# Weight parts in four homes, raw loads seven units ahead, and other distances for x's chunks in a two-layer decoder trunk

## The chip, the cores and the metric

One core of a Trainium2 chip. The metric is the time of one execution in device microseconds (us), the median of the runs shown.

## What is computed

A trunk of two layers on 256 tokens with 2048 features, all in float32. Each layer normalises its input, multiplies it with one wide matrix `w_in`, runs three token mixers on the columns of the product, projects the result of each by its own matrix, weighs the three by sigmoid gates, and adds the product with `w_out` to its input. A last normalisation closes the trunk. Cut to what the change touches:

```python
def hybrid_layer(x, norm_w, w_in, ..., w_a_out, w_b_out, w_c_out, w_out, cos, sin, top_k):
    h = rms_norm(x, norm_w)
    proj = h @ w_in
    ...
    y_b = (conformer_conv(ub, conv_w, conv_b, cln_w, cln_b) * jax.nn.silu(zb)) @ w_b_out
    ...
    g = jax.nn.sigmoid(gates).reshape(b, s, N_BRANCH, D_MODEL)
    merged = g[:, :, 0] * y_a + g[:, :, 1] * y_b + g[:, :, 2] * y_c
    return x + merged @ w_out

def reference(x, ...):
    for i in range(DEPTH):
        x = hybrid_layer(x, norm_w[i], w_in[i], ...)
    return rms_norm(x, final_norm_w)
```

## The kernel before

**Weights.** A float32 product is made of three products of reduced parts: high times high, low times high, high times low. A unit of weights is 256 rows by 512 columns. `load_unit` (L235) has SP load it raw, 512 KB, into one of four raw buffers. ACT casts it into the high part `wh` (`high`, L246), DVE subtracts that from the raw unit and has the low part `wl` (`low`, L250), and PE multiplies: twelve matmuls of 128x512 for a plain unit (L260). `wh` and `wl` have three buffers each, here called homes. A cast into a home waits until PE has used what was there.

**The two pipelines.** Twice in a layer the units are run by `run` (L480 to 510): once for the gates of the second branch with its projection `w_b_out`, and once for `w_out`. Its inner `ahead(n)` gives out the load of unit n + 4 and casts and subtracts unit n + 2, and then unit n is multiplied. Fourteen units of each pipeline come from `seven` (L418 to 476): these are half units (six matmuls) of a product of two by two blocks with seven instead of eight block products. The weights of some are sums of blocks: `fetch` (L439) has SP load the first block into a slot in two halves, and `more` (L454) has POOL add the second by an accumulating transfer. Outside of these pipelines, `unit` loads, casts and subtracts at once, with three homes.

**x's chunks at a layer's end.** The product with `w_out` is made in four quarters of 512 columns. For each quarter `ask` (L1414) has SP load the layer's input chunk, `arrive` (L1447, L1449) has DVE add the product and what `seven` kept aside, and `leave` has ACT square the chunk for the next normalisation (L612). In layer 0 `turned` then takes the chunk to the features' layout: DVE transposes blocks (L289), POOL stores them in four transfers `z` (L292), POOL loads them back as `zy` (L298, one buffer), DVE multiplies with the norm's weight (L617), ACT casts (L624), and DVE subtracts the low part (L173). How many units later the load and the multiplication come is `LATER - 2 - (q == 3)`, with LATER 10, and `least` 3. The scheduler orders the instructions of each engine by such distances and by priorities.

**Layer 1's start.** Layer 1 multiplies raw features first: its norm's factor, one number per token, is made from the squares by L630 and L519 to L524 (ACT's square root is L519), set on diagonals by L537 and L538, and spread over the partitions by two matmuls of PE (L678) in the middle of the sixth unit. The norm's square root needs another function table of ACT than the gates' sigmoids (L1366); `warm_sqrt` (L529) loads it ahead of time.

**The tail.** In layer 1 the quarters' squares give the last norm's factor. The rows of t = 0 are finished first: square root L1534, factor L1535 to L1538, rescale L1544 on DVE and L1542 on ACT, output L1545. Those of t = 1 follow with the merges L1515 and L1525.

Of the kernel before, what the change touches and what calls it, by code (L numbers as in the profile page):

```python
# [8 lines left out]
F32 = mybir.dt.float32  # L9
# [39 lines left out]
def trunk(ctx: ExitStack, tc: tile.TileContext, x, w_in, xt, w_a, w_b, w_c, w_out,  # L49
# [14 lines left out]
    def queued():  # L64
        return tc.issue_after(first[0].ins) if first[0] is not None else nullcontext()

    x0n = cp.tile([P, C_ID + S], F32, name="x0n")
    idle = tp.tile([P, P], F32, tag="dg", bufs=1, name="idle")
    nc.vector.memset(idle, 0.0)
    eps = cp.tile([P, 1], F32, name="eps")  # L70
    nc.vector.memset(eps, EPS)
# [146 lines left out]

    def load_unit(w, k0, kn, segs, dst=None):
        n = sum(c for _, c in segs)  # L220
        raw = wp.tile([P, kn, n], F32, tag="raw", bufs=4, name=nm("raw"))
        if dst is None:
            dst = (wp.tile([P, kn, n], F32R, tag=t, bufs=3, name=nm(t)) for t in ("wh", "wl"))
        count[0] += 1
        with tc.high_priority():
            o = 0
            for c0, c in segs:
                src = w[k0 * P:(k0 + kn) * P, c0:c0 + c].rearrange("(k p) c -> p k c", p=P)
                if count[0] == 1:

                    for k in range(kn):
                        nc.scalar.dma_start(raw[:, k, o:o + c], src[:, k, :])
                else:
                    with queued():
                        dma = nc.sync.dma_start(raw[:, :, o:o + c], src)  # L235
                    if count[0] <= 8:
                        first[0] = dma
                o += c
            if count[0] == 8:
                with queued():  # L240
                    first[0] = nc.sync.dma_start(cst, consts)
        return (raw, *dst)
# [137 lines left out]
    def chunk_N(w, segs, act, nk, ku=2, accs=None, ks=None, banks=False):  # L380
# [4 lines left out]
            background(token_products(accs, n, unit(w, k0, ku, segs), act, k0, ku, nk, range(NT), banks))  # L385
        return accs

    class Unit:

        size, before, now, after = 1, (), (), ()  # L390
# [4 lines left out]
    def plain(w, c0, act, k0, accs, nk, banks=False, ts=range(NT)):  # L395
# [1 line left out]
            return token_products(accs(), 512, u[1:], act, k0, 2, nk, ts, banks)  # L397

        def load():
            u = load_unit(w, k0, 2, [(c0, 512)])  # L400
            count[0] -= 1
            return u

# [17 lines left out]
    def seven(w, c0, act, sums, banks, keep):  # L421
# [19 lines left out]
        def sub(h, g, add, a, k0, t, bank):  # L441
            ts, hs = slice(t * P, (t + 1) * P), slice(h * 2, h * 2 + 2)

            def load():
                if g not in grow:
                    u = load_unit(w, 4 + h * 2, 2, [(c0, 512)])
                    count[0] -= 1
                    return u
                return (grow[g][:, hs, :],
                        *(wp.tile([P, 2, 512], F32R, tag=v, bufs=3, name=nm(v)) for v in ("wh", "wl")))  # L450

            def more():
                with tc.high_priority():
# [23 lines left out]
    def run(units, tasks):  # L477
# [3 lines left out]
        got = {}  # L481

        def ahead(n):
            if n + 4 < len(units):
                for f in units[n + 4].before:
                    f()
                got[n + 4] = units[n + 4].load()
            if 0 <= n + 2 < len(units):
                high(got[n + 2])
                low(got[n + 2])  # L490
                if units[n + 2].more:
                    units[n + 2].more()

        for n in range(-4, 0):
            ahead(n)
        for n, u in enumerate(units):
            ahead(n)
# [149 lines left out]
    for layer in range(DEPTH):  # L647
# [282 lines left out]
        hq = slot(F32R).rearrange("p a (b t) -> p (a b) t", t=P)  # L930
        for v in range(KD // 4):
            nc.scalar.copy(hq[:, v * 4:v * 4 + 4, :].rearrange("p k (w t) -> p k w t", w=2), hx[v][:, :, :, TOPK:P])
        kiT = sp.tile([P, 1, S], F32, tag="kiT", bufs=1, name=nm("kiT"))
        va = [sp.tile([P, NT, 2 * P], F32R, tag=v, bufs=1, name=nm(v)) for v in ("vah", "val")]
        wi = small(NIH, 2)
        wi2 = tp.tile([P, NIH // 2], F32, tag="wi2", bufs=1, name=nm("wi2"))
# [514 lines left out]
        def leave(q):  # L1451
            xc, c0 = xcs[q], q * 512
            x_squares([xc[:, t, :] for t in range(NT)], ssq, q, range(NT))
            if last:
                for t in range(NT):
                    nc.vector.tensor_mul(xfr[t][:, c0:c0 + 512], xc[:, t, :], fwr[:, c0:c0 + 512])
            else:
                turned([xc[:, t, :] for t in range(NT)], partial(x_parts_F, xn, c0 // P, nwn), LATER - 2 - (q == 3),
                       t4() if q == 1 else None, least=3)
                nc.scalar.dma_start(x1[:, :, c0:c0 + 512].rearrange("t p d -> p t d"), xc)  # L1460

        sums = parts(KC)
# [134 lines left out]
```

## Time and profile before

| what | value |
|---|---|
| time, median of 3 runs | 2012.91 us (2012.84 to 2014.74) |
| the profiled execution's own time | 2013.33 us |
| its span in the profile | 2011.6 us |
| PE busy | 2001.1 us, 99% of the span, 9338 matmuls |
| DVE busy | 1595.5 us, 79% |
| ACT busy | 1093.6 us, 54% |
| POOL busy | 210.1 us, 10% |
| share of PE in the chain that ended last | 97% |
| granted TensorE clock | 0.999 of full speed |
| moved by DMA | 463.80 MB, 231 GB/s in the mean |

The span runs from the first to the last record of the profile; the time has some 1.7 us around it. PE, DVE, ACT and POOL are the engines for matmuls, for vector work, for activations and copies, and for transfers with accumulation or a new layout; SP issues most loads. An answer of the timeline has, in each row, the start, the duration, the engine, the line, the operation and its tiles, how many instructions were drawn together, and in brackets how long the engine was idle before and what ended the wait.

### The profile page before, as it was taken

Reading aid. Unit: us, or ns where it says so; the run is one execution under the profiler, and the core shown is the slowest. Engines: PE = TensorE matmul, PEld = TensorE weight load, DVE = VectorE, ACT = ScalarE, POOL = GpSimd, SP = SyncE. Lnnn points to the kernel's source line nnn. Section 1 sums busy time; section 2 is a strip of 40 time slices with the busy share of each in tenths; the row PEclk is TensorE's granted clock in tenths of the full one; section 3 lists DMA queues with packets and bytes.
Section 4 is the critical chain, followed back from the end, with each engine's and each line's share of the span. In section 5 each row is a group of like instructions: output and inputs, shape, how many; then the busy total and the mean of one; then the engine's idle time right before and its main releaser. Section 6 shows DMA issues by size and latency. Waiting matters only on the chain.

```text
span 2011.6 us, 25827 instructions
## 1 busy us (share of the span) xinstructions
PE 2001.1 (99%) x9338; PEld 1677.8 (83%) x9338; DVE 1595.5 (79%) x2124; ACT 1093.6 (54%) x1261; POOL 210.1 (10%) x316
## 2 busy tenths in 40 slices
PE   9999999999999999999999999999999999999998
PEld 8889888888888888888888988888888888888876
DVE  8667899878878876677785779988889788756777
ACT  7556555565644555455564555555656445544564
POOL 0111112100010001212210111111000100012120
PEclk9999999999999999999999999999999999999999
DMA  7788678866676678979987886788666766789795
GB/s 267 230 286 263 189 226 287 246 178 179 180 223 193 182 226 236 279 225 298 290 246 233 278 249 188 234 279 249 178 177 177 221 198 190 226 247 267 235 299 169
DMA packets 235585, 463.80 MB, mean 231 GB/s; under 512 B 17280, under 2 KB 30080, under 8 KB 235328
## 3 DMA queue, kind: packets, MB, share of 16 engines
q1 hardware_dynamic: 206592, 385.06, 62.1%
q0 software_dynamic: 27200, 73.94, 13.9%
q10 hardware_dynamic: 1664, 3.15, 0.4%
q8 instruction: 73, 1.20, 0.3%
q14 instruction: 56, 0.46, 0.1%
HBM read 429.31 MB, written 32.77 MB: 230 GB/s over the span
## 4 chain that ended last, share of the span: by engine, by line
PE 97%; DMA 2%; DVE 0%; ACT 0%; issue 0%; POOL 0%; DVEq 0%; ACTq 0%; POOLq 0%
PE acc L260 84%; PE mm L260 10%; DMA raw<-in_w_out_dram 1%; PE mm L1036 1%; DMA z<-zt 1%; PE mm L1126 0%; DMA zy<-z 0%; PE mm L1094 0%; PE mm L1231 0%; PE mm L1177 0%; ACT wh L246 0%; PE mm L795 0%; PE mm L1207 0%; PE mm L1097 0%; PE mm L1006 0%; PE mm L1236 0%
## 5 line engine op out<-in xcount | busy, mean ns | idle before, releaser
L260 PE MATMUL acc<-wh,s 128*128 128x512 f32 (+1 forms) x5088 | 1259.7, 389 | 1.4 <-ACT wh L246 1.0
L246 ACT CAST wh<-raw 128x1024 fp32r<-128x1024 f32 (+1 forms) x698 | 730.8, 1048 | 767.3 <-PE acc L260 510.8
L260 PEld LDWEIGHTS acc<-wh,s 128*128 128x128 f32 x5088 | 946.9, 188 | 190.9 <-ACT wh L246 2.4
L250 DVE TENSOR_TENSOR wl<-raw,wh 128x1024 fp32r<-128x1024 f32 (+1 forms) x699 | 846.4, 1214 | 319.6 <-ACT wh L246 317.1
L260 PE MATMUL acc<-wl,s 128*128 128x512 f32 (+1 forms) x2352 | 626.2, 388 | 0.0
L260 PEld LDWEIGHTS acc<-wl,s 128*128 128x128 f32 x2352 | 440.8, 188 | 90.2 <-DVE wl L250 1.0
L292 POOL DMA_DIRECT2D z<-zt x196 | 117.6, 616 | 1250.2 <-DVE zt L289 907.6
L605 DVE SCALAR_TENSOR_TENSOR s<-yT,cst,s 128x256 f32<-128x256 f32 x480 | 212.2, 478 | 0.0
L260 PE MATMUL mm<-wh,s 128*128 128x512 f32 x480 | 123.6, 389 | 0.1
L260 PEld LDWEIGHTS mm<-wh,s 128*128 128x128 f32 x480 | 90.0, 188 | 19.2 <-ACT wh L246 0.5
L250 DVE TENSOR_TENSOR wl<-s,wh 128x1024 fp32r<-128x1024 f32 x48 | 58.5, 1219 | 18.4 <-ACT wh L246 18.1
L246 ACT CAST wh<-s 128x1024 fp32r<-128x1024 f32 x48 | 50.5, 1053 | 40.8 <-PE acc L260 22.9
L260 PEld LDWEIGHTS mm<-s,wl 128*128 128x128 f32 x512 | 66.9, 191 | 5.0
L260 PE MATMUL mm<-wl,s 128*128 128x512 f32 x240 | 68.8, 390 | 0.0
L260 PE MATMUL mm<-s,wl 128*128 128x192 f32 x512 | 66.0, 271 | 0.0
L298 POOL DMA_DIRECT2D zy<-z x50 | 36.0, 720 | 268.7 <-DMA z<-zt 140.8
L260 PEld LDWEIGHTS mm<-wl,s 128*128 128x128 f32 x240 | 45.0, 188 | 9.7 <-DVE wl L250 0.4
L289 DVE STREAM_TRANSPOSE zt<-acc 128x512 f32<-128x512 f32 (+1 forms) x68 | 45.4, 681 | 8.2 <-PE acc L260 8.2
L454 POOL DMA_DIRECT2D s<-in_w_in_dram x16 | 19.2, 1203 | 115.7 <-DVE wl L250 100.8
L543 DVE TENSOR_TENSOR s<-zy,s 128x1024 fp32r<-128x1024 f32 x20 | 24.3, 1215 | 5.1 <-ACT s L542 5.1
L542 ACT CAST s<-zy 128x1024 fp32r<-128x1024 f32 x20 | 21.0, 1048 | 11.8 <-DVE zy L593 7.0
L1313 DVE TENSOR_TENSOR ev<-acc,ev 128x512 f32<-128x512 f32 x24 | 16.5, 688 | 11.9 <-PE acc L260 11.9
(280 smaller groups left out, 1093.4 us busy)
## 6 DMA issues: line engine op xcount, KB each, us to landing
raw<-in_w_in_dram SPq DMA_DIRECT2D x539, 512.0 KB, 4.5
raw<-in_w_out_dram SPq DMA_DIRECT2D x52, 512.0 KB, 7.2
zy<-z POOLq DMA_DIRECT2D x48, 512.0 KB, 5.2
z<-zt POOLq DMA_DIRECT2D x188, 128.0 KB, 4.6
raw<-in_w_a_dram SPq DMA_DIRECT2D x32, 512.0 KB, 3.9
raw<-in_w_c_dram SPq DMA_DIRECT2D x32, 512.0 KB, 4.4
raw<-in_w_b_dram SPq DMA_DIRECT2D x32, 512.0 KB, 5.0
s<-in_w_in_dram POOLq DMA_DIRECT2D x16, 512.0 KB, 8.3
```

What stands on the lines that cost most here:

```text
L246: newest_parts[0] = nc.scalar.copy(u[1], u[0])
L250: newest_parts[1] = sub = nc.vector.tensor_sub(u[2], u[0], u[1].bitcast(F32))
L260: newest[0] = nc.tensor.matmul(o, lhsT, rhs, start=start, stop=stop, skip_group_check=True)
L289: nc.vector.transpose(tmp[:, t].rearrange("p b k i -> p k b i"), src.rearrange("p k (b c) -> p k b c", b=4, c=32))
L292: nc.gpsimd.dma_start(z[:, :, :, a, :].rearrange("t b c e -> c (t b) e"), tmp[a * 32:(a + 1) * 32].rearrange("c t b k i -> c (t b) (k i)"))
L298: nc.gpsimd.dma_start(y.rearrange("p (t a) k i -> p t (a k i)", a=4), z.rearrange("t b c a e -> (b c) t (a e)"))
L454: nc.gpsimd.dma_start(grow[g][:, hs, :], block(add, h), accum_op=ALU.add)
L542: nc.scalar.copy(h, src)
L543: nc.vector.tensor_sub(l, src, h.bitcast(F32))
L605: nc.vector.scalar_tensor_tensor(o, yT[:, c, q:q + S], wq, o, op0=ALU.mult, op1=ALU.add)
L1036: nc.tensor.matmul(ps[:, q * S:(q + 1) * S], qi[i][:, hd, :], ki[j][:, 0, :], start=n == 0, stop=n == 2)
L1313: nc.vector.tensor_mul(sg[t], y[t], sg[t])
```

## The change

Raw units have five buffers instead of four. A new helper `weight_parts` gives the two pipelines their homes: every fourth is a pair of tiles `ph`, `pl`, which other code uses in other stages, so there are four instead of three. `ahead` loads seven units ahead instead of four and converts three ahead instead of two. To make room in the on-chip memory, `x0n`, `idle` and `kiT` move into buffers whose tags other tiles have. For x's chunks the distance `LATER - 2 - (q == 3)`, which is 8, 8, 8, 7, becomes `LATER - (5, 4, 2, 3)[q]`, which is 5, 6, 8, 7, and `least` becomes 4 for the third chunk.

```diff
--- before.py
+++ after.py
@@ -64,8 +64,8 @@
     def queued():
         return tc.issue_after(first[0].ins) if first[0] is not None else nullcontext()
 
-    x0n = cp.tile([P, C_ID + S], F32, name="x0n")
-    idle = tp.tile([P, P], F32, tag="dg", bufs=1, name="idle")
+    x0n = sp.tile([P, C_ID + S], F32, tag="yT", bufs=1, name="x0n")
+    idle = tp.tile([P, P], F32, tag="sc", bufs=2, name="idle")
     nc.vector.memset(idle, 0.0)
     eps = cp.tile([P, 1], F32, name="eps")
     nc.vector.memset(eps, EPS)
@@ -218,7 +218,7 @@
 
     def load_unit(w, k0, kn, segs, dst=None):
         n = sum(c for _, c in segs)
-        raw = wp.tile([P, kn, n], F32, tag="raw", bufs=4, name=nm("raw"))
+        raw = wp.tile([P, kn, n], F32, tag="raw", bufs=5, name=nm("raw"))
         if dst is None:
             dst = (wp.tile([P, kn, n], F32R, tag=t, bufs=3, name=nm(t)) for t in ("wh", "wl"))
         count[0] += 1
@@ -385,6 +385,15 @@
             background(token_products(accs, n, unit(w, k0, ku, segs), act, k0, ku, nk, range(NT), banks))
         return accs
 
+    homes = [0]
+
+    def weight_parts():
+
+        homes[0] += 1
+        if homes[0] % 4 == 0:
+            return [v.rearrange("p (k c) -> p k c", k=2) for v in pair(1024)]
+        return [wp.tile([P, 2, 512], F32R, tag=t, bufs=3, name=nm(t)) for t in ("wh", "wl")]
+
     class Unit:
 
         size, before, now, after = 1, (), (), ()
@@ -397,7 +406,7 @@
             return token_products(accs(), 512, u[1:], act, k0, 2, nk, ts, banks)
 
         def load():
-            u = load_unit(w, k0, 2, [(c0, 512)])
+            u = load_unit(w, k0, 2, [(c0, 512)], weight_parts())
             count[0] -= 1
             return u
 
@@ -443,11 +452,10 @@
 
             def load():
                 if g not in grow:
-                    u = load_unit(w, 4 + h * 2, 2, [(c0, 512)])
+                    u = load_unit(w, 4 + h * 2, 2, [(c0, 512)], weight_parts())
                     count[0] -= 1
                     return u
-                return (grow[g][:, hs, :],
-                        *(wp.tile([P, 2, 512], F32R, tag=v, bufs=3, name=nm(v)) for v in ("wh", "wl")))
+                return (grow[g][:, hs, :], *weight_parts())
 
             def more():
                 with tc.high_priority():
@@ -481,17 +489,17 @@
         got = {}
 
         def ahead(n):
-            if n + 4 < len(units):
-                for f in units[n + 4].before:
+            if n + 7 < len(units):
+                for f in units[n + 7].before:
                     f()
-                got[n + 4] = units[n + 4].load()
-            if 0 <= n + 2 < len(units):
-                high(got[n + 2])
-                low(got[n + 2])
-                if units[n + 2].more:
-                    units[n + 2].more()
-
-        for n in range(-4, 0):
+                got[n + 7] = units[n + 7].load()
+            if 0 <= n + 3 < len(units):
+                high(got[n + 3])
+                low(got[n + 3])
+                if units[n + 3].more:
+                    units[n + 3].more()
+
+        for n in range(-7, 0):
             ahead(n)
         for n, u in enumerate(units):
             ahead(n)
@@ -930,7 +938,7 @@
         hq = slot(F32R).rearrange("p a (b t) -> p (a b) t", t=P)
         for v in range(KD // 4):
             nc.scalar.copy(hq[:, v * 4:v * 4 + 4, :].rearrange("p k (w t) -> p k w t", w=2), hx[v][:, :, :, TOPK:P])
-        kiT = sp.tile([P, 1, S], F32, tag="kiT", bufs=1, name=nm("kiT"))
+        kiT = tp.tile([P, S], F32, tag="rb", bufs=1, name=nm("kiT")).unsqueeze(1)
         va = [sp.tile([P, NT, 2 * P], F32R, tag=v, bufs=1, name=nm(v)) for v in ("vah", "val")]
         wi = small(NIH, 2)
         wi2 = tp.tile([P, NIH // 2], F32, tag="wi2", bufs=1, name=nm("wi2"))
@@ -1455,8 +1463,8 @@
                 for t in range(NT):
                     nc.vector.tensor_mul(xfr[t][:, c0:c0 + 512], xc[:, t, :], fwr[:, c0:c0 + 512])
             else:
-                turned([xc[:, t, :] for t in range(NT)], partial(x_parts_F, xn, c0 // P, nwn), LATER - 2 - (q == 3),
-                       t4() if q == 1 else None, least=3)
+                turned([xc[:, t, :] for t in range(NT)], partial(x_parts_F, xn, c0 // P, nwn), LATER - (5, 4, 2, 3)[q],
+                       t4() if q == 1 else None, least=3 + (q == 2))
                 nc.scalar.dma_start(x1[:, :, c0:c0 + 512].rearrange("t p d -> p t d"), xc)
 
         sums = parts(KC)
```

The lines of the changed kernel are eight or nine higher: L617 is L625, L439 is L448, L1414 is L1422, L1447 is L1455.

How the order moves, at three places. First SP's queue in layer 0's second pipeline: raw weight loads (L235), the two halves of a fetch (L439, L448) and the request for x's last chunk (L1414, L1422). Before:

```order
L235 DMA raw_1364_7792<-in_w_out_dram 128x2x512
L235 DMA raw_1367_7812<-in_w_out_dram 128x2x512
L1414 DMA t4_1445_8225<-in_x_dram 128x2x512
L235 DMA raw_1372_7830<-in_w_out_dram 128x2x512
L439 DMA s8_1371_7827<-in_w_out_dram 128x2x512
L235 DMA raw_1377_7860<-in_w_out_dram 128x2x512
L235 DMA raw_1382_7889<-in_w_out_dram 128x2x512
```

and now:

```order
L235 DMA raw_1362_7743<-in_w_out_dram 128x2x512
L235 DMA raw_1366_7764<-in_w_out_dram 128x2x512
L235 DMA raw_1373_7799<-in_w_out_dram 128x2x512
L448 DMA s8_1370_7794<-in_w_out_dram 128x2x512 x2
L1422 DMA t4_1442_8177<-in_x_dram 128x2x512
L235 DMA raw_1378_7829<-in_w_out_dram 128x2x512
L235 DMA raw_1384_7862<-in_w_out_dram 128x2x512
```

The ninth unit's load, raw_1372 before and raw_1373 now, stood behind the request for x's chunk; it now stands ahead of it, and both halves of the fetch stand together.

Second, DVE at the end of layer 0, from the merge of x's third chunk (t4_1429) on: weights' low parts (L250), transposes (L289), the first chunk's multiplication (L617, now L625) and low part (L173). Before:

```order
L1449 TENSOR_TENSOR t4_1429_8149<-t4_1429_8149,s8_1339_7704 128x512
L250 TENSOR_TENSOR wl_1458_8280<-raw_1456_8277,wh_1457_8279 128x1024
L289 STREAM_TRANSPOSE zt_1463_8333<-t4_1429_8149 128x4x4x32 x2
L250 TENSOR_TENSOR wl_1461_8298<-raw_1459_8295,wh_1460_8297 128x1024
L617 TENSOR_TENSOR s8_1465_8368<-zy_1452_8257,cst_75 128x1024
L250 TENSOR_TENSOR wl_1480_8416<-raw_1478_8413,wh_1479_8415 128x1024
L173 TENSOR_TENSOR s8_1466_8370<-s8_1465_8368,s8_1466_8370 128x4x256
L250 TENSOR_TENSOR wl_1483_8420<-raw_1481_8417,wh_1482_8419 128x1024
```

and now:

```order
L1457 TENSOR_TENSOR t4_1429_8112<-t4_1429_8112,s8_1339_7704 128x512
L625 TENSOR_TENSOR s8_1462_8318<-zy_1461_8271,cst_75 128x1024
L250 TENSOR_TENSOR pl_1456_8242<-raw_1457_8243,ph_1455_8241 128x1024
L250 TENSOR_TENSOR wl_1482_8422<-raw_1480_8419,wh_1481_8421 128x1024
L250 TENSOR_TENSOR wl_1485_8426<-raw_1483_8423,wh_1484_8425 128x1024
L173 TENSOR_TENSOR s8_1463_8320<-s8_1462_8318,s8_1463_8320 128x4x256
L289 STREAM_TRANSPOSE zt_1466_8342<-t4_1429_8112 128x4x4x32
L250 TENSOR_TENSOR wl_1490_8436<-raw_1488_8433,wh_1489_8435 128x1024
L289 STREAM_TRANSPOSE zt_1466_8342<-t4_1429_8112 128x4x4x32
L625 TENSOR_TENSOR s8_1462_8318<-zy_1464_8322,cst_75 128x1024
```

The first chunk's L625, three L250 and its L173 now stand ahead of the third chunk's first transpose, and another L250 ahead of the second; before, one L250 stood ahead of both.

Third, DVE at the start of layer 1, from the transposes of the last chunk on: the sum of the squares (L630, now L638) opens the chain of the norm's factor. Before:

```order
L289 STREAM_TRANSPOSE zt_1469_8394<-t4_1445_8225 128x4x4x32 x2
L630 TENSOR_REDUCE sm_1497_8487<-sm_1334_7699 128x2
L520 TENSOR_SCALAR sm_1498_8489<-sm_1497_8487 128x2
L521 RECIPROCAL sm_1498_8489<-sm_1498_8489 128x2
L522 TENSOR_TENSOR sm_1498_8489<-sm_1498_8489 128x2
L523 SCALAR_TENSOR_TENSOR sm_1498_8489<-sm_1498_8489 128x2
L524 SCALAR_TENSOR_TENSOR sm_1498_8489<-sm_1498_8489 128x2
L537 TENSOR_SCALAR ph_1499_8496<-cst_75,sm_1498_8489 128x128
L538 SCALAR_TENSOR_TENSOR pl_1500_8497<-cst_75,sm_1498_8489,ph_1499_8496 128x128
```

and now:

```order
L289 STREAM_TRANSPOSE zt_1471_8400<-t4_1442_8177 128x4x4x32 x2
L625 TENSOR_TENSOR s8_1497_8487<-zy_1469_8378,cst_75 128x1024
L638 TENSOR_REDUCE sm_1500_8493<-sm_1334_7699 128x2
L528 TENSOR_SCALAR sm_1501_8495<-sm_1500_8493 128x2
L529 RECIPROCAL sm_1501_8495<-sm_1501_8495 128x2
L530 TENSOR_TENSOR sm_1501_8495<-sm_1501_8495 128x2
L531 SCALAR_TENSOR_TENSOR sm_1501_8495<-sm_1501_8495 128x2
L532 SCALAR_TENSOR_TENSOR sm_1501_8495<-sm_1501_8495 128x2
L545 TENSOR_SCALAR ph_1502_8502<-cst_75,sm_1501_8495 128x128
```

The third chunk's L625 now stands ahead of the chain; before, its L617 came behind the chain and one L250.

On ACT, the last gate sigmoids of the first pipeline (L1366, now L1374) now come behind `warm_sqrt`, and ACT_TABLE_LOAD stands at four more places: at these sigmoids in both layers, ahead of the square root L519 (now L527) at layer 1's start, and in the tail right ahead of the square root L1534 (now L1542) of the first half.

## Rows read from the trace of the kernel before

**Rows 1.** Timeline of PE at the layers' boundary; its columns are given above

```profile
1007.83 1.07 PE L260 MATMUL acc<-wl,s 128*128 128x512 f32 x4
1008.74 1.07 PE L260 MATMUL acc<-wh,s 128*128 128x512 f32 x4
1010.07 1.20 PE L260 MATMUL acc<-wh,s 128*128 128x512 f32 x4 [0.26 <-DVE s L173]
```

**Rows 2.** Timeline of PE in the second pipeline of layer 0

```profile
936.97 0.61 PE L260 MATMUL mm<-wl,s 128*128 128x512 f32 x2
937.89 2.11 PE L260 MATMUL acc<-wh,s 128*128 128x512 f32 x8 [0.30 <-ACT wh L246]
939.83 1.07 PE L260 MATMUL acc<-wl,s 128*128 128x512 f32 x4
```

**Rows 3.** Timeline of PE in the second pipeline of layer 1

```profile
1935.70 0.61 PE L260 MATMUL mm<-wl,s 128*128 128x512 f32 x2
1937.05 2.14 PE L260 MATMUL acc<-wh,s 128*128 128x512 f32 x8 [0.74 <-ACT wh L246]
...
1940.85 0.61 PE L260 MATMUL mm<-wl,s 128*128 128x512 f32 x2
1941.54 2.11 PE L260 MATMUL mm<-wh,s 128*128 128x512 f32 x8
```

**Rows 4.** Timeline of PE in the first pipelines, of layer 0 and of layer 1

```profile
798.91 0.61 PE L260 MATMUL mm<-wh,s 128*128 128x512 f32 x2
799.48 1.20 PE L260 MATMUL acc<-wl,s 128*128 128x512 f32 x4
...
1860.04 1.07 PE L260 MATMUL acc<-wl,s 128*128 128x512 f32 x4
1861.20 2.11 PE L260 MATMUL acc<-wh,s 128*128 128x512 f32 x8
```

**Rows 5.** Timeline of SP and of ACT ahead of the stall of rows 2

```profile
928.66 0.37 SPq L235 DMA_DIRECT2D raw<-in_w_out_dram  x1
...
936.79 1.05 ACT L246 CAST wh<-raw 128x1024 fp32r<-128x1024 f32 x1 [4.34 <-DMA raw<-in_w_out_dram]
```

**Rows 6.** Timeline of ACT at the warming square root of layer 1

```profile
1913.77 1.28 ACT L529 ACT_TABLE_LOAD   x1
1915.07 0.20 ACT L529 ACTIVATE sm<-eps 128x1 f32<-128x1 f32 x1
```

**Rows 7.** Timeline of DVE in the tail

```profile
2000.65 1.28 DVE L1544 TENSOR_SCALAR s<-s,sm 128x256 f32<-128x256 f32 x3
2002.22 0.69 DVE L1515 TENSOR_TENSOR t<-acc,t 128x512 f32<-128x512 f32 x1 [0.29 <-PE acc L260]
...
2003.48 0.42 DVE L1528 TENSOR_TENSOR s<-t,s 128x256 f32<-128x256 f32 x1
```

**Rows 8.** Timeline of DVE at the layers' boundary

```profile
995.69 1.30 DVE L289 STREAM_TRANSPOSE zt<-t 128x512 f32<-128x512 f32 x2
...
1005.91 1.22 DVE L617 TENSOR_TENSOR s<-zy,cst 128x1024 f32<-128x1024 f32 x1 [0.59 <-DMA zy<-z]
...
1013.61 0.12 DVE L630 TENSOR_REDUCE sm<-sm 128x2 f32<-128x8 f32 x1
...
1016.11 1.22 DVE L250 TENSOR_TENSOR wl<-raw,wh 128x1024 fp32r<-128x1024 f32 x1
```

**Rows 9.** Timeline of POOL at the layers' boundary

```profile
999.52 0.72 POOL L298 DMA_DIRECT2D zy<-z  x1 [1.09 <-DVE s L617]
...
1007.81 0.72 POOL L298 DMA_DIRECT2D zy<-z  x1 [6.39 <-DMA z<-zt]
...
1019.80 0.72 POOL L298 DMA_DIRECT2D zy<-z  x1 [3.48 <-DVE wl L250]
```

**Rows 10.** Timeline of PE behind the spread of the norm's factor

```profile
1019.50 1.09 PE L260 MATMUL acc<-wl,s 128*128 128x512 f32 x4
```

**Rows 11.** Windows: us, busy time (instructions) of each engine, granted clock, DMA share, GB/s

```profile
930.00:970.00 40.00, 39.70 (x176) 32.55 (x175) 27.58 (x26) 21.84 (x23) 8.15 (x8) 1.00 1.07 293
```

## The prediction

> **What bounds the kernel now.** The chain of waits in the page runs almost wholly over PE, and the time slices show PE full in all but the last. So I read PE's own timeline for places where a matmul starts late. Undisturbed, four 128x512 matmuls take 0.91 us [rows 1]: 0.227 us each, so a unit of twelve takes 2.72 us and a half unit (six) 1.36 us. A start that comes later than the start before it plus 0.227 us per matmul is a stall, and its size is the first thing the reader is to see in [rows 1 to 4]. A stall has a second part: the matmuls just behind it run slower. The eight that start at 937.89 end at 939.83, 1.94 us instead of 1.82 [rows 2]. I put 0.12 us on every stall for that.
>
> **What may be gained.** Each stall is worked out so.
> - Layer boundary [rows 1]: 1008.74 + 0.91 = 1009.65, the matmul starts at 1010.07, released by DVE's L173, the low part of x's second chunk: 0.42 + 0.12 = 0.54.
> - Second pipeline, layer 0 [rows 2]: 936.97 + 0.45 = 937.42 against 937.89: 0.47 + 0.12 = 0.59.
> - Second pipeline, layer 1 [rows 3]: 1935.70 + 0.45 = 1936.15 against 1937.05: 0.90 + 0.12 = 1.02; and 1940.85 + 0.45 = 1941.30 against 1941.54: 0.24 + 0.12 = 0.36.
> - First pipeline, layer 0 [rows 4]: 798.91 + 0.45 = 799.36 against 799.48: 0.24 with the 0.12. Layer 1 has the same start at 1797.80: together 0.48.
> - First pipeline, layer 1 [rows 4]: 1860.04 + 0.91 = 1860.95 against 1861.20: 0.37.
>
> The sum is 3.36 us. Two more starts of some 0.2 us (1953.58, 1958.82) I leave out of the sum. That is the whole prize, and it is under 0.2% of the time (4.0 us), which is about what a measurement of this kernel can tell from no change. Faster by more than that is hardly open to this change, since it takes no matmul away.
>
> **Does the change reach these stalls?** The matmuls keep their order but for the entry of the first pipeline. What moves is when a unit's weights are ready.
> - The stalls in the second pipeline. The cast at 936.79 waited 4.34 us for a raw weight load that SP had issued at 928.66, 8.1 us before [rows 5]; SP issued it so late because a raw buffer had to come free, and x's request stood ahead of it. The order now has this load (raw_1373) ahead of the two halves of the fetch and of x's request. It needs only a conversion that lies three units instead of two before its use, and a fifth buffer. That is at least one unit earlier, 1.36 to 2.72 us, against 0.47 and 0.90 us of lateness. I count all three as gone.
> - The first pipeline. Every cast now waits for a matmul unit one earlier, so cast and subtraction run 1.36 to 2.72 us sooner, against 0.12 and 0.25 us of lateness. Gone. The extra casts cost ACT nothing: it does the same number of casts.
> - The boundary stall. L625 for the second chunk now stands ahead of the last chunk's merge with its L173 right behind it, and its load is issued ahead of all four stores of the third chunk. Gone.
>
> Moving x0n, idle and kiT to other buffers adds no instruction. Their first writers come long after the buffers are free, so I cost this at nothing; if that cover were gone, it would show as a wait at the head of the program or in the sparse branch.
>
> **What it costs: the tail.** The order for ACT has an added ACT_TABLE_LOAD ahead of the final square root, because the last gate sigmoids moved behind the warming square root. A load takes 1.28 us [rows 6]. The rescale of the first half starts at 2000.65 and takes 1.28 [rows 7]; 1.28 later it ends at 2003.21, and the merge that starts at 2002.22 is 0.99 late. The two merges of 256 columns now stand ahead of the product with the weight (0.42 us [rows 7]) that stood between them, so 0.99 - 0.42 = 0.57 us is what I take; the bounds are 0 and 1.28. The same load also stands ahead of the square root at layer 1's start, without a wait of its own, where ACT has idle time: nothing. Rows show a switch of tables as 1913.77 to 1915.07, 1.30 us from the load's start to the next instruction, with nothing behind it [rows 6]. The Trainium skill (ScalarE: Activation LUTs, What ACT_TABLE_LOAD costs) adds a drain of about 1.38 us to each switch, 2.66 us in all; by that the tail would lose some 1.4 us more. Rows show no such drain here; I keep it as a rival.
>
> **What it costs: layer 1's first normalisation.** This is the term that decides. Before, DVE transposed the third chunk at 995.69, and it was done at 996.99 [rows 8]. In the new order five more 1024-column steps stand ahead of or between these two transposes (L625, two L250, L173, and one L250 between): 5 x 1.22 = 6.1 us [rows 8], so they end at 1003.1, and up to 2.72 later if an L250 there waits a unit for its cast. POOL then issues the stores, done by 1004.6 (before, the last of them was out at 1007.81 - 6.39 = 1001.42, with another load between them [rows 9]; I take 1.5 us after the transposes). From the last store to the load zy the trace has 3.48 us in one case and 6.39 in the other [rows 9]; the second may be the buffer, since L617 (1005.91 + 1.22 = 1007.13) freed it just before. I take 4.3, nearer to the shorter. The load takes 6.39 us, from 999.52 to 1005.91 [rows 8, 9]. So the chunk lands at 1004.6 + 4.3 + 6.4 = 1015.3.
>
> That would cover itself, were it not that its L625 now stands **ahead** of the sums of squares and the whole rsqrt chain, which before came first (L617 behind it). So: L625 1.22, the chain from 1013.61 to 1016.11 2.50 [rows 8], L250 of the sixth unit 1.22: the low part is ready at 1020.2. PE wanted it at 1019.50 [rows 10], now 0.54 earlier: 1018.96. A stall of 1.3 us. Bounds: with 3.48 for the store 0.4, and below that nothing; with 6.39 and the 2.72 of a late cast 6.1.
>
> **Sum.** 2013.33 (the profiled execution: span 2011.6 and 1.7 around it) - 3.36 + 0.57 + 1.3 = **2011.8 us**. That execution is 0.42 above the median of the three runs shown, 2012.91, well inside their spread.
>
> **The rivals.**
> - *The boundary costs more than all the rest gives* (the other side). Place: DVE's L625 for the third chunk ahead of the rsqrt chain. Price: up to 6.1 - 3.36 + 0.57, that is 2016.6; in its middle 2014.5. It decides from the point where that chunk lands after 1016.8 (1015.3 plus the 1.5 that the forecast is ahead). For it: both waits of this chain are of 6.4 us in the trace [rows 9]. Against: the chain lies in a stretch where fewer loads run than in the pipeline.
> - *The gains do not come, as the loads are bound by the DMA engines.* From 930 to 970 us their busy share is 1.07, at 293 GB/s [rows 11]. Then an earlier issue makes an earlier transfer of one load by delaying another, and the three stalls of the second pipelines (0.59 + 1.02 + 0.36 = 1.97) stay somewhere: 2013.8. Against: in the 8.1 us of [rows 5] SP waited for a buffer before it issued the load, and that part of the wait is not the engines'. The Trainium skill (DMA: Bandwidth & Descriptors, Issuing engines are not separate DMA queues) says that transfers of all issuers run on the same 16 engines and interleave; the trace agrees in that POOL's and SP's bytes add up in this share.
> - *All goes right.* The chunk lands before the last chunk's transposes are through, the table load hides: 2013.33 - 3.36 = 2010.0.
> - *The drain of the table switch*: 2011.8 + 1.4 = 2013.2.
>
> **Chances.** Forecast 0.52, boundary 0.18, DMA bound 0.12, all right 0.15, drain 0.03. The range reaches from the all-right case, a little below it for the two starts left out, to the middle of the boundary case and half a microsecond on: 2009.7 to 2015.0. Faster by over 0.2% needs 2008.9 and lies below all cases: 0.03 for what I overlook. Slower by over 0.2% needs 2016.9, only the end of the boundary case and what I overlook: 0.05. Within 0.2%: 0.92.
>
> **What would show it.** Right: no PE start late near 799, 937, 1010, 1861, 1937 and 1941; the cast of the ninth unit in the second pipeline without a wait for a w_out load; one more table load ahead of the last square root and the tail from the last matmul to the end about half a microsecond longer; a stall of about a microsecond at the sixth unit of layer 1, released by DVE. Wrong: that stall at 3 us or more, or a new wait of PE in the pipelines for ACT or for x's chunks, which would mean that what the loads gained was taken from other transfers.

## The result, and the profile after

The changed kernel takes 2038.93 us (median of 4 runs, 2036.89 to 2040.14) against 2012.88 before; the ratio is 1.0127, 95% interval 1.0109 to 1.0145. It is 26 us slower, where 2011.8 was forecast and 2015.0 was the top of the range. The profiled execution took 2038.21 us, with a span of 2036.5, 24.9 more than before. In the runs further down one execution, of shift32, took 3756.54 us at a granted clock of 0.811; the ratios leave it out.

The page of the changed kernel (first its line for PE, then PE's share of the chain, then two of the costliest groups with their mean ns of one):

```profile
PE 2023.5 (99%) x9338; PEld 1680.5 (83%) x9338; DVE 1599.2 (79%) x2124; ACT 1099.7 (54%) x1265; POOL 210.2 (10%) x316
PE 99%; DVE 1%; ACT 0%; issue 0%; DVEq 0%
L260 PE MATMUL acc<-wh,s 128*128 128x512 f32 (+1 forms) x4848 | 1213.5, 392 | 0.0
L260 PE MATMUL acc<-wl,s 128*128 128x512 f32 (+1 forms) x2232 | 600.2, 391 | 0.7 <-DVE wl L250 0.7
```

The same groups on the page of before:

```profile
L260 PE MATMUL acc<-wh,s 128*128 128x512 f32 (+1 forms) x5088 | 1259.7, 389 | 1.4 <-ACT wh L246 1.0
L260 PE MATMUL acc<-wl,s 128*128 128x512 f32 (+1 forms) x2352 | 626.2, 388 | 0.0
```

PE is as full as before. Its idle time is 2036.5 - 2023.5 = 13.0 us, and was 2011.6 - 2001.1 = 10.5: waits explain 2.5 of the 24.9 us. The other 22.4 are busy time: in these two groups one matmul is 3 ns longer in the mean, 392 for 389 and 391 for 388. No view of waits can show that. The timeline of PE shows it from start to start, in a stretch of layer 0 that the change does not touch. Before:

```profile
258.93 1.98 PE L260 MATMUL acc<-wh,s 128*128 128x512 f32 x8
260.74 1.07 PE L260 MATMUL acc<-wl,s 128*128 128x512 f32 x4
261.65 1.98 PE L260 MATMUL acc<-wh,s 128*128 128x512 f32 x8
```

and after:

```profile
262.19 2.03 PE L260 MATMUL acc<-wh,s 128*128 128x512 f32 x8
264.06 1.10 PE L260 MATMUL acc<-wl,s 128*128 128x512 f32 x4
264.99 1.33 PE L260 MATMUL acc<-wh,s 128*128 128x512 f32 x5
```

Twelve matmuls took 261.65 - 258.93 = 2.72 us, 0.227 each; now they take 264.99 - 262.19 = 2.80 us, 0.233 each, with no gap between them. Over all 8126 matmuls of 128x512 the mean from start to start in the records (starts over 300 ns left out) is 227.2 ns before and 230.2 after: 8126 x 3.0 = 24 us. The granted clock is 0.999 in both.

**What the forecast spoke of** is there beside it. The stalls of [rows 1 to 4] are gone, all of them. One new one stands in the second pipeline of layer 1, where the low part of a unit in the fourth home comes late. PE's timeline, and DVE's:

```profile
1952.08 2.01 PE L260 MATMUL acc<-ph,s 128*128 128x512 f32 x8
1954.80 1.21 PE L260 MATMUL acc<-pl,s 128*128 128x512 f32 x4 [0.70 <-DVE pl L250]
```

```profile
1951.20 1.30 DVE L289 STREAM_TRANSPOSE zt<-s 128x512 f32<-128x512 f32 x2
1952.42 1.18 DVE L551 TENSOR_TENSOR s<-zy,s 128x1024 fp32r<-128x1024 f32 x1
1953.53 1.22 DVE L250 TENSOR_TENSOR pl<-raw,ph 128x1024 fp32r<-128x1024 f32 x1
```

Eight matmuls from 1952.08 end near 1953.93, the next starts at 1954.80: 0.9 us, as two transposes and a subtraction (L551) stand ahead of L250 on DVE. And the stall at layer 1's start is there. PE, DVE, ACT and POOL around it:

```profile
1028.84 1.99 PE L260 MATMUL acc<-wh,s 128*128 128x512 f32 x8
1032.53 0.38 PE L686 MATMUL mm<-ph,ones_r 128*128 128x256 f32 x1 [1.70 <-DVE ph L545]
1032.92 0.38 PE L686 MATMUL mm<-pl,ones_r 128*128 128x256 f32 x1
1034.05 1.21 PE L260 MATMUL acc<-wl,s 128*128 128x512 f32 x4 [0.75 <-DVE wl L250]
```

```profile
1026.33 1.23 DVE L625 TENSOR_TENSOR s<-zy,cst 128x1024 f32<-128x1024 f32 x1 [2.26 <-DMA zy<-z]
1027.47 0.15 DVE L638 TENSOR_REDUCE sm<-sm 128x2 f32<-128x8 f32 x1
...
1030.82 0.17 DVE L529 RECIPROCAL sm<-sm 128x2 f32<-128x2 f32 x1 [2.99 <-ACT sm L527]
...
1032.78 1.22 DVE L250 TENSOR_TENSOR wl<-raw,wh 128x1024 fp32r<-128x1024 f32 x1
```

```profile
1028.13 1.05 ACT L246 CAST wh<-raw 128x1024 fp32r<-128x1024 f32 x1 [1.70 <-PE acc L260]
1029.19 1.28 ACT L527 ACT_TABLE_LOAD   x1
1030.49 0.30 ACT L527 ACTIVATE sm<-sm,eps 128x2 f32<-128x2 f32 x1
```

```profile
1020.88 0.72 POOL L298 DMA_DIRECT2D zy<-z  x1 [3.60 <-DVE t L1457]
```

The eight matmuls from 1028.84 are followed at 1030.67 by nothing: L686 starts 1.86 late, its second matmul 0.27, and L260 1.0, in all 3.1 us for the forecast's 1.3. From the last store to the load it was 3.60 (forecast 4.3), and the load took 1026.33 - 1020.88 = 5.45 (6.39). The chain took more: from L638 to L250 it is 1032.78 - 1027.47 = 5.31 us, where before it was 2.50 [rows 8]. ACT holds it: a cast that waited for PE, and behind it the table load, which I had costed at nothing, stand ahead of the square root (L527), and DVE waits 2.99 us for that.

So the 24.9 us are 24.2 from the matmuls' pace, 3.1 at layer 1's start, 0.9 in the second pipeline and 0.8 in the tail (from PE's last row, 2002.02 + 1.59 before and 2026.15 + 1.59 now, to the end of the span: 8.0 and 8.8), less some 4 of stalls gone (the 3.36 of the forecast and the two starts that it left out, 0.4).

### The profile page after: what moved, and what is told of

Read it like the earlier page. It is cut to its first block, busy times and chain, and to the rows that moved or that the text cites. A ratio compares the mean times of both kernels' runs of the same rounds, so it can differ in the third digit from the quotient of the medians.

```text
span 2036.5 us, 25835 instructions
## 1 busy us (share of the span) xinstructions
PE 2023.5 (99%) x9338; PEld 1680.5 (83%) x9338; DVE 1599.2 (79%) x2124; ACT 1099.7 (54%) x1265; POOL 210.2 (10%) x316
## 4 chain that ended last, share of the span: by engine, by line
PE 99%; DVE 1%; ACT 0%; issue 0%; DVEq 0%
PE acc L260 85%; PE mm L260 11%; PE mm L1044 1%; PE mm L1134 0%; PE mm L1239 0%; PE mm L1102 0%; PE mm L1185 0%; PE mm L803 0%; PE mm L1215 0%; PE mm L1244 0%; PE mm L1014 0%; PE mm L1188 0%; PE mm L1105 0%; DVE s L1552 0%; PE mm L1217 0%
## 5 line engine op out<-in xcount | busy, mean ns | idle before, releaser
L260 PE MATMUL acc<-wh,s 128*128 128x512 f32 (+1 forms) x4848 | 1213.5, 392 | 0.0
L246 ACT CAST wh<-raw 128x1024 fp32r<-128x1024 f32 (+1 forms) x659 | 689.7, 1048 | 746.5 <-PE acc L260 603.2
L260 PEld LDWEIGHTS acc<-wh,s 128*128 128x128 f32 x4848 | 903.5, 188 | 189.3 <-ACT wh L807 0.3
L250 DVE TENSOR_TENSOR wl<-raw,wh 128x1024 fp32r<-128x1024 f32 (+1 forms) x660 | 799.4, 1214 | 305.2 <-ACT wh L246 301.8
L260 PE MATMUL acc<-wl,s 128*128 128x512 f32 (+1 forms) x2232 | 600.2, 391 | 0.7 <-DVE wl L250 0.7
L260 PEld LDWEIGHTS acc<-wl,s 128*128 128x128 f32 x2232 | 419.2, 188 | 91.8 <-DVE wl L250 0.9
L260 PE MATMUL mm<-wh,s 128*128 128x512 f32 x392 | 102.2, 393 | 0.0
L260 PEld LDWEIGHTS mm<-wh,s 128*128 128x128 f32 x392 | 73.6, 188 | 16.3
L260 PEld LDWEIGHTS mm<-s,wl 128*128 128x128 f32 x512 | 67.0, 191 | 5.5
L250 DVE TENSOR_TENSOR wl<-s,wh 128x1024 fp32r<-128x1024 f32 x42 | 51.4, 1223 | 22.7 <-ACT wh L246 22.6
L260 PE MATMUL mm<-s,wl 128*128 128x192 f32 x512 | 66.1, 271 | 0.0
L250 DVE TENSOR_TENSOR pl<-raw,ph 128x1024 fp32r<-128x1024 f32 x39 | 47.6, 1221 | 20.4 <-ACT ph L246 20.4
L260 PE MATMUL acc<-ph,s 128*128 128x512 f32 x240 | 60.4, 393 | 0.0
L246 ACT CAST ph<-raw 128x1024 fp32r<-128x1024 f32 x39 | 40.9, 1048 | 33.0 <-DVE wl L250 10.0
L260 PE MATMUL mm<-wl,s 128*128 128x512 f32 x196 | 56.7, 391 | 0.0
L260 PEld LDWEIGHTS acc<-ph,s 128*128 128x128 f32 x240 | 45.0, 188 | 10.2
L289 DVE STREAM_TRANSPOSE zt<-acc 128x512 f32<-128x512 f32 (+1 forms) x68 | 45.4, 681 | 10.2 <-PE acc L260 10.2
L260 PEld LDWEIGHTS mm<-wl,s 128*128 128x128 f32 x196 | 36.8, 188 | 8.4
```

The lines of the kernel that those rows point to most:

```text
L246: newest_parts[0] = nc.scalar.copy(u[1], u[0])
L250: newest_parts[1] = sub = nc.vector.tensor_sub(u[2], u[0], u[1].bitcast(F32))
L260: newest[0] = nc.tensor.matmul(o, lhsT, rhs, start=start, stop=stop, skip_group_check=True)
L289: nc.vector.transpose(tmp[:, t].rearrange("p b k i -> p k b i"), src.rearrange("p k (b c) -> p k b c", b=4, c=32))
```

## The experiments

Two theories at the start. **Addresses**: the moves of x0n, idle and kiT and the fifth raw buffer shift everything behind them in the on-chip memory, and the pace of a matmul hangs on where its operands lie. **Loads or order**: more casts and loads ahead, or other waits, disturb PE. The addresses, per partition, are those that the compiled programs hold: before, all weight parts (`wh`, `wl`) and all slots with activations (`s8`, printed `s` in the rows) start 32 bytes past a multiple of 512; in the changed kernel weight parts start at 416 and slots at 352. The sizes of the tiles give the same, and say why. `x0n` has 288 floats, 1152 bytes, which is 128 past a multiple of 512: without it everything behind lies 128 lower, at 416. In its new place it opens the buffer `yT` ahead of the slots, 8 x 286 floats or 9152 bytes, 448 past a multiple of 512: 416 + 448 - 512 = 352. `idle` (512 bytes), `kiT` (1024) and a raw buffer (4096) are whole multiples. By this sum `x0n` alone makes the difference; no run moved it alone.

**moved_only.** Only the three tiles move; the order on PE, ACT, POOL and SP is that of before. Weight parts come to 416 and slots to 352, as in the change.

```diff
-    x0n = cp.tile([P, C_ID + S], F32, name="x0n")
-    idle = tp.tile([P, P], F32, tag="dg", bufs=1, name="idle")
+    x0n = sp.tile([P, C_ID + S], F32, tag="yT", bufs=1, name="x0n")
+    idle = tp.tile([P, P], F32, tag="sc", bufs=2, name="idle")
...
-        kiT = sp.tile([P, 1, S], F32, tag="kiT", bufs=1, name=nm("kiT"))
+        kiT = tp.tile([P, S], F32, tag="rb", bufs=1, name=nm("kiT")).unsqueeze(1)
```

> The kernel before with x0n, idle and kiT moved as in the change, and nothing else: four raw buffers, the old distances, the same order on PE, ACT, POOL and SP. Only addresses in the on-chip memory differ: the weight parts start at 416 and the activation slots at 352 bytes past a multiple of 512, as in the changed kernel; before both start at 32. Theory of addresses (each matmul starts later because of where its operands lie): 8126 matmuls of 128x512 at about 230 instead of 227 ns, 24 us more, 2036 to 2040 us. Theory of the loads (more loads and casts ahead disturb PE's reads): 2013 us, 227 ns. Theory of the order (what waits changed): 2013 us.

Measured: 2037.14 us against 2013.69 on the same chip, ratio 1.0116 (1.0087 to 1.0146), 230.2 ns: 23.5 of the 26 us come with the three tiles alone.

**after_pads.** The changed kernel and two unused tiles; the order stays.

```diff
+    cp.tile([P, 32], F32, name="pad_c")
     x0n = sp.tile([P, C_ID + S], F32, tag="yT", bufs=1, name="x0n")
+    sp.tile([P, 16], F32, tag="pad", bufs=1, name="pad_s")
```

> The changed kernel with two unused tiles of 128 and 64 bytes ahead of the raw buffers and of the slots, so that weight parts and slots start again at 32 bytes past a multiple of 512; the order and all distances are those of the change. Theory of addresses: 227 ns a matmul, and of the changed kernel's 2038 us some 24 go: 2011 to 2015, what its order alone is worth. Theory of the loads or of the order: 2036 to 2040, 230 ns.

Measured: 2015.03, ratio 1.0007 (0.9996 to 1.0018), 227.1 ns. 192 bytes that nobody reads give 24 us back. The order and the loads ahead are still there, so they are not what slows a matmul. What is left is what the forecast was about, and its sum cannot be told from nothing. One thing is added at layer 1's start. PE's timeline, then windows (us, busy time of PE, PEld, DVE, ACT and POOL, granted clock, DMA share, GB/s):

```profile
1019.53 0.39 PE L688 MATMUL mm<-ph,ones_r 128*128 128x256 f32 x1 [1.72 <-DVE ph L547]
1019.91 0.39 PE L688 MATMUL mm<-pl,ones_r 128*128 128x256 f32 x1
1021.05 1.22 PE L262 MATMUL acc<-wl,s 128*128 128x512 f32 x4 [0.75 <-DVE wl L252]
1022.07 3.57 PE L262 MATMUL acc<-wh,s 128*128 128x512 f32 x8
1025.48 1.09 PE L262 MATMUL acc<-wl,s 128*128 128x512 f32 x4
```

```profile
1016.00:1022.00 6.00, 3.53 (x14) 2.35 (x14) 3.97 (x10) 3.99 (x6) 0.72 (x1) 1.00 0.39 126
1022.00:1026.00 4.00, 4.00 (x13) 3.09 (x12) 4.00 (x5) 0.41 (x2) 0.00 (x0) 0.57 0.83 251
```

Behind the stall eight matmuls take 1025.48 - 1022.07 = 3.41 us instead of 1.81, at a granted clock of 0.57 over the window: close to the lower of the two levels, 1.2 GHz. PE had been busy for 3.53 of the 6 us before. The stall costs 3.2 and 1.6 us more. In the profiled executions of the changed kernel and of after_pad64 a stall of the same size cost no clock; in that of order_only it did again. The Trainium skill (TensorE: Matmul & The Clock Gate, Part 1) says that the clock falls to half after the engine has been idle; the trace agrees here, and those of the changed kernel and of after_pad64 do not show it.

**before_shift, shift64, shift32.** The kernel before with one unused tile ahead of the raw buffers, 384, 64 or 32 bytes (`cp.tile([P, 96], F32, name="pad_c")`, 16 or 8 in place of 96). Weight parts and slots move together.

> The kernel before with one unused tile of 384 bytes ahead of the raw buffers: same instructions in the same order, every buffer 384 bytes further, so weight parts and slots both start at 416 past a multiple of 512, and as before at the same place of a multiple of 2048. Theory of addresses, if the place in 512 bytes counts: 230 ns, 2036 to 2040 us. If what counts is that weight parts and slots lie alike: 227 ns, 2013 us. Theory of the loads or the order: 2013 us.

> The kernel before with one unused tile of 64 bytes ahead of the raw buffers: weight parts and slots both come to 96 past a multiple of 128. Theory of relative place: 227 ns, 2013 us. Theory of absolute place: 230 ns or more, 2037 us.

> The kernel before with one unused tile of 32 bytes ahead of the raw buffers: weight parts and slots both lie at multiples of 64, where before they lay 32 past one. Theory of relative place: 227 ns and 2013 us, as they still lie alike. If a row that starts inside 64 bytes costs a read more, matmuls get faster: 223 to 226 ns, 1980 to 2005 us. Theory of absolute place: open, as no run has had this place.

Measured: 2014.42 (ratio 1.0002, 0.9991 to 1.0013), 2013.70 (1.0003, 0.9992 to 1.0013) and 2015.32 (1.0008, 0.9997 to 1.0019), 227.2 ns in all three. So where both operands lie alike their absolute place does not count, and a place at 0 of 64 bytes helps nothing: the hope of 223 to 226 ns failed.

**slots64, and slots32, 128, 192, 256, 384.** The kernel before with one unused tile ahead of the slots alone, so that only the distance from weight parts to slots changes.

```diff
+    sp.tile([P, 16], F32, tag="pad", bufs=1, name="pad_s")
     idle = tp.tile([P, P], F32, tag="dg", bufs=1, name="idle")
```

> The kernel before with one unused tile of 64 bytes ahead of the slots alone: weight parts stay at 32 past a multiple of 128, the slots with the activations come to 96. Same instructions in the same order, nothing else moves but what lies behind the slots. Theory of relative place (a matmul is slow where its two operands lie 64 bytes apart in 128): 229 to 233 ns, about 2037 us. Theory of absolute place (an operand at 96 in 128 is slow): the same here. Theory that only the moved tiles x0n, idle and kiT matter: 2013 us.

> The kernel before with one unused tile of 32 bytes ahead of the slots: weight parts at 32 past a multiple of 64, slots at 0, 32 bytes apart in 512. Theory that only 64 bytes or more apart counts: 227 ns, 2013 us. Theory that any difference of place counts, and grows with it: between 227 and 233 ns, 2025 to 2050 us.

> The kernel before with one unused tile of 128 bytes ahead of the slots: operands 128 bytes apart in 512. Theory of a period of 128 bytes: 227 ns, 2013 us. Theory of a period of 512 bytes: not 227 ns, 2030 to 2070 us, or, if some distance is better than none, below 2013.

> The kernel before with one unused tile of 256 bytes ahead of the slots: operands 256 bytes apart in 512, as far as they can be. Theory of a period of 128 or 256 bytes: 227 ns, 2013 us. Theory of a period of 512 bytes: not 227 ns, 2030 to 2070 us, or below 2013 if some distance is better than none.

> The kernel before with one unused tile of 192 bytes ahead of the slots. Theory of a period of 256 bytes in the distance of the operands: as in moved_only, where slots lie 448 (192 and 256) past the weight parts: 229 to 231 ns, 2030 to 2042 us. Theory of a period of 512: open, 227 to 235 ns.

> The kernel before with one unused tile of 384 bytes ahead of the slots. Theory of a period of 256 bytes: as slots128, 232.6 ns, about 2055 us. Theory of a period of 512: as far from 0 as 128 is on the other side, so perhaps the same, perhaps 227 to 230 ns.

| slots past weight parts, modulo 512 | run | ns, start to start | us |
|---|---|---|---|
| 0 | before | 227.2 | 2012.88 |
| 32 | slots32 | 233.5 | 2062.17 |
| 64 | slots64 | 233.4 | 2060.33 |
| 128 | slots128 | 232.6 | 2054.93 |
| 192 | slots192 | 229.9 | 2033.60 |
| 256 | slots256 | 227.2 | 2012.29 |
| 384 | slots384 | 232.7 | 2054.64 |
| 448 | moved_only | 230.2 | 2037.14 |

The kernel before took 2013.18 to 2014.05 us (medians) on the chips of these runs. PE's timeline of slots64 in the stretch shown above, and at its end:

```profile
260.70 2.03 PE L261 MATMUL acc<-wh,s 128*128 128x512 f32 x8
262.57 1.09 PE L261 MATMUL acc<-wl,s 128*128 128x512 f32 x4
263.50 2.03 PE L261 MATMUL acc<-wh,s 128*128 128x512 f32 x8
...
2038.99 9.70 PE L261 MATMUL acc<-s,s 128*128 128x512 f32 x42
2048.53 1.59 PE L261 MATMUL mm<-s,s 128*128 128x256 f32 x12
```

2.80 us for twelve, with the instructions and the order of before. In the same execution 42 matmuls whose operands both lie in slots took 2048.53 - 2038.99 = 9.54 us, 0.227 each: so a matmul of the same shape keeps the old pace where both operands lie in the slots. What counts is the distance, with a period of 256 bytes: 384 is like 128, 448 like 192, 256 like 0. Two expectations were too low: slots64 was to take about 2037 us, and slots32 at most 2050. slots32 also fell out against the expectation that only 64 bytes or more count, and slots128 against a period of 128. No distance was faster than 0. The runs of 32, 128, 192, 256 and 384 are single ones; the steps of 20 to 48 us are large against the spread of 5 us of the kernel before.

**order_only.** The change's order with the addresses of before: four raw buffers, loads six ahead instead of seven, the three tiles unmoved. Only the fourth home lies elsewhere: `ph` starts at 480 of 512, so slots lie 64 past it.

> The change without its memory: four homes, casts three units ahead, loads six units ahead (the most that four raw buffers give), x's new distances, and x0n, idle, kiT where they were, so every address is that of the kernel before. Theory of addresses: 227 ns a matmul and 2010 to 2014 us. Theory of the loads: 229 to 230 ns and 2028 to 2040 us. Theory of the order: 2036 to 2040 us.

Measured: 2024.09, ratio 1.0054 (1.0031 to 1.0077), between the theories. PE's timeline in the first pipeline says why:

```profile
804.78 1.98 PE L260 MATMUL acc<-wh,s 128*128 128x512 f32 x8
806.59 1.07 PE L260 MATMUL acc<-wl,s 128*128 128x512 f32 x4
807.50 1.09 PE L260 MATMUL mm<-ph,s 128*128 128x512 f32 x4
808.43 0.63 PE L260 MATMUL mm<-pl,s 128*128 128x512 f32 x2
808.90 2.00 PE L260 MATMUL acc<-wh,s 128*128 128x512 f32 x8
810.73 1.07 PE L260 MATMUL acc<-wl,s 128*128 128x512 f32 x4
811.64 1.98 PE L260 MATMUL acc<-wh,s 128*128 128x512 f32 x8
```

A whole unit takes 807.50 - 804.78 = 2.72, 0.227 each. The half unit from the fourth home takes 808.90 - 807.50 = 1.40, 0.233 each; the eight matmuls behind it 1.83, 0.229 each; then the pace is back. So the pace goes with the home that is multiplied, and a slow unit still slows the matmuls behind it. In the mean over all matmuls of 128x512 it is 227.7 ns, 0.5 more than before, or 4 us. The rest is the stall at layer 1's start, with a slow clock behind it as in after_pads, and one stall of 3.6 us in the second pipeline of layer 1, where a raw load was late. ACT, then PE, then a window:

```profile
1945.79 1.04 ACT L246 CAST ph<-raw 128x1024 fp32r<-128x1024 f32 x1 [7.34 <-DMA raw<-in_w_out_dram]
```

```profile
1946.88 3.78 PE L260 MATMUL acc<-ph,s 128*128 128x512 f32 x8 [3.44 <-ACT ph L246]
```

```profile
1947.00:1953.00 6.00, 6.00 (x15) 4.70 (x16) 5.03 (x5) 3.72 (x4) 2.44 (x2) 0.53 0.65 191
```

Behind the stall the granted clock is 0.53, and eight matmuls take 3.78 us, where 1.98 is usual. With four raw buffers and loads six ahead this stall is there; with five and seven it is not.

**after_pad64.** The changed kernel with one unused tile of 64 bytes ahead of the slots: slots and the fourth home come to 416, where the other weight parts are.

> The changed kernel with one unused tile of 64 bytes ahead of the slots, so that slots and the fourth home start 416 bytes past a multiple of 512 as the other weight parts do; nothing else is changed. Theory of the distance: 227 ns, and 2013 to 2016 us, the stall at layer 1's start stays. Theory that the place in 512 counts too (32 there, 416 here): between 2016 and 2038.

Measured: 2014.57, ratio 1.0008 (0.9996 to 1.0019), 227.1 ns. The 64 bytes of distance are the whole difference in pace, and weight parts at 416 are as good as at 32.

**pads_old_x.** after_pads with x's distances of before.

```diff
-                turned(..., LATER - (5, 4, 2, 3)[q], t4() if q == 1 else None, least=3 + (q == 2))
+                turned(..., LATER - 2 - (q == 3), t4() if q == 1 else None, least=3)
```

> The changed kernel with the two unused tiles that bring the operands to 32 past a multiple of 512, and x's distances as before (LATER - 2 - (q == 3), least 3), so that the sum of squares and the chain of the norm's factor stand ahead of L617's successor for the third chunk again. Theory that this placing makes the stall at layer 1's start and the slow clock behind it (1.9 + 0.3 + 1.0 and eight matmuls 0.2 us late, 4.8 us in the run with the two tiles): that stall goes, 2015.0 - 4.8 = about 2010. Rival, that the new homes and casts three units ahead make it: it stays, 2014 to 2016. In either case a stall at the boundary for the second chunk's low part may come back (0.5 us).

Measured: 2013.65, ratio 1.0002 (0.9993 to 1.0012). The stall at L688 is gone, and the one of [rows 1] is back and larger:

```profile
1007.92 1.09 PE L262 MATMUL acc<-wh,s 128*128 128x512 f32 x4
1011.13 1.20 PE L262 MATMUL acc<-wh,s 128*128 128x512 f32 x4 [2.11 <-DVE s L175]
```

2.3 us (1011.13 - 1007.92 - 0.91), where I had put 0.5. On DVE the second chunk is multiplied at 1005.42, and three merges of the product and a weights' low part run before its own low part at 1009.86; in the kernel before, it was one low part and one merge. So with the pipelines of the change the old distances are late for the second chunk, and the new ones bring the stall at layer 1's start; the distances were not tried one at a time. A table load stands ahead of the square root here too (1012.51), and PE does not wait for the chain: with an earlier chain the load costs nothing.

**pads_best.** after_pads with both: the first two chunks as in the change, the third multiplied later, and the table loaded behind the last sigmoids.

```diff
-        warm_sqrt()
+        tasks.append(warm_sqrt)
...
-                turned(..., LATER - (5, 4, 2, 3)[q], t4() if q == 1 else None, least=3 + (q == 2))
+                turned(..., LATER - (5, 4, 1, 3)[q], t4() if q == 1 else None, least=3 + 2 * (q == 2))
```

> The changed kernel with the two unused tiles; x's distances LATER - (5, 4, 1, 3)[q] with least 5 for the third chunk, so that the second chunk's low part comes as early as in the change and the third chunk's multiplication behind the norm's chain; and the warming square root put at the end of the second pipeline's tasks, so that no table load stands in the tail. Theory (relative place, the order of L617's successor, the table load are all that was wrong): no stall over 0.3 us in the pipelines or at the boundary, 227 ns a matmul, no load in the tail: 3.4 us under the kernel before, 2009 to 2011. Rival, that casts three units ahead cost elsewhere: 2012 to 2015.

Measured: 2011.05 (11 runs) against 2014.05 (15 runs of the kernel before on the same chip), ratio 0.9986 (0.9976 to 0.9995): 0.14% faster than the kernel before, with the whole interval under 1. The two edits were not tried apart. Its waits, all that the view of PE's waits has, and its timeline at layer 1's start:

```profile
PE mm L805 <- DVE eps L73: 1.1, 1, 1.1
PE acc L262 <- DVE pl L252: 0.3, 1, 0.3
```

```profile
1016.24 1.98 PE L262 MATMUL acc<-wh,s 128*128 128x512 f32 x8
1018.05 0.28 PE L688 MATMUL mm<-ph,ones_r 128*128 128x256 f32 x1
1018.16 0.28 PE L688 MATMUL mm<-pl,ones_r 128*128 128x256 f32 x1
1018.28 1.09 PE L262 MATMUL acc<-wl,s 128*128 128x512 f32 x4
```

The spread of the norm's factor starts as the matmul before it is through. The gain is 3.0 us by the medians and 3.3 by the spans (2008.3 against 2011.6), near the 3.36 that the forecast had worked out as the prize.

## Why the prediction was wrong

- **The step that failed** is the one that cost the moves of x0n, idle and kiT at nothing because they add no instruction. moved_only shows 23.5 us for these moves alone; slots64 shows the mechanism without them, and after_pad64 takes it back with 64 bytes. I had looked at what the tiles' users wait for and not at what moves behind the tiles: the slots came to lie 64 bytes before the weight parts, modulo 512. No rival had it, and the list of what would show the forecast wrong spoke of waits alone. One of its signs did come, the stall at layer 1's start at 3 us or more, but it is 3.1 of the 26 us.
- **Pipelines**: all the stalls I counted as gone went, in the changed kernel and in after_pads. The term of 3.36 was right; a new stall of 0.9 us at a low part in the fourth home I had not seen.
- **Layer 1's start**: place and releaser were right, the size was not, 3.1 for 1.3. The term that failed is the chain of 2.50 us: with a cast and the table load ahead of the square root on ACT it took 5.31, 2.8 more. I had called that load free. The term that I held to decide, the chunk's landing, was if anything too long: the store and the load together took 1.6 us less than forecast.
- **The tail**: 0.57 forecast, 0.8 measured; right in kind, as ACT's timeline has the table load at 2023.74, right ahead of the last norm's square root.
- **The drain of a table switch**: at 1029.19 the load began and the square root followed at 1030.49, 1.30 later. No drain in these rows either.
- **DMA bound**: the three stalls of the second pipelines went at a DMA share of 1.03 to 1.05 (930 to 980 us in layer 0, 1945 to 1995 in layer 1), hardly lower than [rows 11]; this rival fell. Casts of ACT still wait for raw loads there (3.20 us at 948.75), but three units ahead of use PE does not notice.

With the addresses put right, the change as it stands is worth nothing that can be measured (after_pads, after_pad64): 4 us of stalls go, and some 5 come at layer 1's start, in the second pipeline and in the tail. So without the addresses too the forecast of 2011.8 would have been some 3 us low.

## What to carry to other kernels

A tile that is moved, added or resized moves every tile behind it, and on this kernel that alone costs from nothing to some 48 us: compare the addresses of the matmuls' two operands before and after, modulo 256, as one compares the order. If a kernel gets slower by more than its waits explain, look at the mean of one instruction and at the time from start to start in a stretch that the change does not touch. A distance that relieves one chain puts its work ahead of another; undo such numbers one at a time.

## What was not expected of the hardware

Matmuls of 128x512 whose moving weight part and stationary activations start at the same place modulo 256 bytes followed each other every 226.7 ns in undisturbed stretches; at distances of 32 to 128 bytes the mean was 232.6 to 233.5, at 192 about 230. Matmuls of 128x192 and of 128x400 do not show it: the median from start to start is 111 to 112 and 179 to 182 ns at every distance of the table.

A slow unit slows what is behind it: in order_only the half unit took 0.04 us longer and the eight matmuls behind it 0.02. In the changed kernel the units of the fourth home, which lie at distance 0 from the slots between units at 448, were slow too. In the mean over their whole units the last two of the twelve matmuls ran at 227.0 and 226.7 ns, and the first of the next unit at 235 to 237. That fits a delay which the units before leave behind and which ends within the unit; no run tried it. Nor is it shown why a distance costs anything.
